# Gates and values of a hybrid attention layer: token-major seven-product blocks in place of weight pairs

## The chip, the cores and the metric

The kernel runs on one core of a Trainium2 chip. The metric is the device time of one launch in microseconds (us). Engines are called by the profile's names: PE is TensorE (matmuls), DVE is VectorE, ACT is ScalarE, POOL is GpSimd and SP is the engine that issues most DMAs.

## The reference, cut to what matters

One layer on 512 tokens of width 2048, float32. One projection of the normalised input makes nine things; two token mixers, latent attention (A) and a spatial gating unit (B), are gated, added and projected.

```python
h = rmsnorm(x, attn_norm_g) * (1 + scale) + shift        # shift, scale, gate = silu(c) @ w_ada + b_ada
q_lat, kv_lat, k_rope, z_mla, u, v, z_sgu, g_mla, g_sgu = split_cols(h @ w_in)   # 768 512 64 and six of 2048
y_mla = causal_mla_attention(...) * silu(z_mla)          # 16 heads of 128, softmax over 512 keys
y_sgu = u * (tril(w_s) @ rmsnorm(v) + b_s) * silu(z_sgu) # 16 groups of 128 columns, chunks of 128 tokens
merged = sigmoid(g_mla) * y_mla + sigmoid(g_sgu) * y_sgu
x = x + gate * (merged @ w_out); return rmsnorm(x)
```

In the kernel the column groups are called by letters: z and g are `z_mla` and `g_mla` (16 heads of 128 columns each), u, s and t are `u`, `z_sgu` and `g_sgu`, v is `v`.

## The kernel before, in words

**Arithmetic.** Every float32 operand is split into a high part (a cast, on ACT) and a low part (a subtraction, on DVE), both in the type `fp32r`; a product is three matmuls, high by high, high by low and low by high (`mm3`, lines 143 to 146). A weight granule of 1024 columns therefore costs one ACT cast and one DVE subtraction before PE can use it. `Stream` (`ws`) loads, splits and hands out granules in a fixed order, one granule split ahead and three loaded ahead.

**Stages on PE, in order.** (1) `g1`: 16 granules for the first 1024 columns of `w_in` (the latents). (2) `g2`: 16 granules for 640 columns. Beside these two, DVE computes the dot products of silu(c) with `w_ada` (`ada_dot`, one 128x2048 tile each) and `fix_to` turns the inputs into the final h, split into `hh[j]`, `hl[j]`. (3) The plain stage (`gb`): two granules of 1024 columns for g of head 14, and v's upper 1024 columns with `k_rope`'s 64 in three column groups of 384, 384 and 320 columns, tokens on the partitions. Four more dots (`NG = 4`) run here. (4) The blocks: seven `BLOCKS`, each a 2x2 block product done with seven products in place of eight. A block takes two groups of 512 columns, for instance v's first two. Its list `V7` has 28 slots; in a slot a weight granule meets 12 matmuls of 512 columns, with tokens stationary (token-major: tokens on the partitions of the result). The sums of h's quarters that the seven products need are made once (`make_sums`, `sums`). (5) The pairs: 14 pairs of weight granules (`PAIRS`), z or g of two neighbouring heads, by the same seven products, but with the weights stationary and 256 tokens moving, 98 slots of 24 or 16 matmuls; the result has features on the partitions, as attention wants it. (6) Attention, head by head. (7) The output projection in four column groups of 512 with the residual, gate and final norm; twelve more dots of the gate run here.

**Who orders the rest.** The order is written out by hand and nothing reorders it. In stages 4 and 5 small jobs (mixing of B, rotary tables, norms of the latents, biases from `shift`) are put into slots by `on(slot, phase, f)`; `place` looks for a slot in which the DVE time noted so far leaves room. Slots of the blocks count up to -1, those of the pairs from 0. In a slot the phases run in the order FIRST, HIGH (cast of the granule of two slots later), EVAC, GATE, SPLIT (its low part), BACK, then the matmuls, then MISC and LOAD. `lat_split` makes the high and low parts of the ten latent tiles that attention reads.

**Attention for one head.** `scores`, `softmax` (mask, maximum and exponentials; `normalise` multiplies the probabilities by 1/sum on DVE), the next head's query projection (`qproj`, and for even heads the rotary part of the next pair, `rproj`), ten `transposes` of the probabilities and their splits, `kproj` of the next head, `turn` (four transposes of B's part), `pv`, `merge_a` (times the gate `gt[h]`, plus B's part), and for odd heads `vproj`. The banks of PSUM go round in a ring of seven.

Of the kernel before, what the change touches and what calls it, by code (L numbers as in the profile page):

```python
# [37 lines left out]
GATED = "ust"  # L38
VW = (384, 384, 320)
VC = (1024, 1408, 1792)  # L40
# [7 lines left out]
DOTS = (3, 3, 4, 5, 5, 6, 7, 8, 9, 9, 10, 11, 11, 12, 12, 13, 13, 14, 14, 15, 16, 16, 16, 16, 16)  # L48
FIXED = (0, 0, 0, 0, 2, 2, 2, 2, 2, 4, 4, 4, 6, 6, 8, 8, 10, 10, 12, 12, 14, 14, 16, 16, 16)

SHIFT_AT = (17, 18, 19, 20, 21, 22, 23, 24, 25, 27, 28, 30, 31, 33, 34, 36)

# [13 lines left out]
class Stream:  # L66
# [17 lines left out]
    def dma_to(self, i):  # L84
        i = min(i, len(self.src) - 1 if self.limit is None else self.limit)
        while self.n_dma <= i:
            k = self.n_dma
            for f in self.before.pop(k, ()):
                f()
            ap, n, _ = self.src[k]  # L90
            pool, tag = self.raws[self.next_raw]
            self.next_raw = (self.next_raw + 1) % len(self.raws)
            t = pool.tile([P, GW], F32, tag=tag, name=f"{tag}_{k}")
            for o, m, ap_ in ap if isinstance(ap, list) else [(0, n, ap)]:
                (self.first if k == 0 else self.nc.sync).dma_start(t[:, o:o + m], ap_)
            self.raw[k] = t
            self.n_dma += 1
# [27 lines left out]
def trunk_layer(ctx, tc, xT, xn, c, vecs, pos, wada, w1, w2, wv, wv3, wv4, wh, wh15, wq, wqr, wk, wvv, wo, wsT, bsp, gfin, out,  # L125
# [82 lines left out]
    ssv = nt(cst, [P, NB, 5], F32, "ssv")  # L208
    rv = nt(cst, [P, NB], F32, "rv")
    cosT = nt(latp.p, [P, S], F32, "cosT")  # L210
# [9 lines left out]
    z_d = scratch("z_d", [P, S])  # L220
    v_d = scratch("v_d", [NB, P, D])
    kr_d = scratch("kr_d", [NB, P, 64])
# [4 lines left out]
    g_d = [scratch(f"g_d{i}", [8, P, S]) for i in range(2)]  # L227
# [34 lines left out]
    def third_place():  # L262
        return [nt(c1[0].p, [P, GW], F32R, tag) for tag in ("w2h", "w2l")]


    steps = [("z", 0)] + [(0, i) for i in range(8)] + [("z", 1)] + [(cg, i) for cg in (1, 2) for i in range(8)]
    gb = []
    for cg, i in steps:
        if cg == "z":
            gb.append(ws.add(wh[H - 2, 1, i], GW))  # L270
        else:
            last = (cg, i) == (2, 7)
            gb.append(ws.add((wv3[0], wv3[1], wv4)[cg][i], 2 * VW[cg], to=third_place if last else None))
# [41 lines left out]
    ada = Scope("ada", side=RIGHT)  # L315
    xp = Scope("xT")
# [25 lines left out]
    xt = [nt(xp.p, [P, S], F32, f"x{j}") for j in range(KC)]  # L342
# [29 lines left out]
    for j in range(NG):  # L372
        load_before(gb[8 + j], ada_load, 2 * KC + j)
# [5 lines left out]
    def square_of(j):  # L379
# [3 lines left out]
        sq = nt(xp.p, [P, S], F32, "sq", bufs=2)  # L383
# [58 lines left out]
    n_fix = 0  # L442

    def fix_to(n, between=None):

        nonlocal n_fix
        if n_fix >= min(n, KC):
            if between:
                between()
            return  # L450
        js = range(n_fix, min(n, KC))
        assert n_dot >= js[-1] + 1
        n_fix = js[-1] + 1
        cols = slice(js[0], n_fix)
        tt(shift[:, cols], dots[:, cols], vec[:, C_BADA + js[0]:C_BADA + n_fix], ALU.add)
        ts_ = []
        for j in js:
            t = nt(xp.p, [P, S], F32, "t", bufs=2)
            stt(t, xt[j], gxA[:, j:j + 1], rx, ALU.mult, ALU.mult)
            ts_.append(t)  # L460
        for j, t in zip(js, ts_):
            hh[j] = nt(hp.p, [P, S], F32R, f"hh{j}")
            ACT.activation(hh[j], t, AF.Identity, bias=shift[:, j:j + 1])
        if between:
            between()
        for j, t in zip(js, ts_):
            hl[j] = nt(hp.p, [P, S], F32R, f"hl{j}")
            stt(hl[j], t, shift[:, j:j + 1], hh[j].bitcast(F32), ALU.add, ALU.subtract)

    ws.split_to(g2[0])  # L470
    for m in range(8):
        ACT.copy(lat[m], ps1[m])
# [7 lines left out]
    for j in range(KC):  # L480
        wH, wL = get(g2[j])
# [3 lines left out]
        if j < NB:  # L485
            DVE.reciprocal(out=rx[:, j * P:(j + 1) * P], in_=rx[:, j * P:(j + 1) * P])
        dot_to(DOTS[j])
        fix_to(FIXED[j])
    for m in range(5):
        pend.append(lambda m=m: ACT.copy(lat[8 + m], ps2[m]))  # L490
# [7 lines left out]
    def parts_of(name, c):  # L498

        if name in sums:  # L500
            return sums[name][:, c, 0], sums[name][:, c, 1]
        return sums[name + "h"][:, c], sums[name + "l"][:, c]

    def split_sum(name, j, src):
        hilo(*parts_of(name, j), src)

    def half_of(tags, j):

        if j % 2 == 0:
            halves_[tags, j // 2] = slot(tags[j // 2])  # L510
        return halves_[tags, j // 2][:, (left, right)[j % 2]]

    halves_, s3f, s4f = {}, {}, {}
    S3_AT, S4_AT = ("lat8", "lat9", "lat12", "lat7"), ("lat0", "lat1", "lat2", "lat3")

    def make_sums(j):
        a, b = (nt(tb.p, [P, S], F32, f"t{i}") for i in range(2))
        tt(a, hh[j].bitcast(F32), hl[j].bitcast(F32), ALU.add)
        tt(b, hh[j + 8].bitcast(F32), hl[j + 8].bitcast(F32), ALU.add)
        s3f[j], s4f[j] = half_of(S3_AT, j), half_of(S4_AT, j)  # L520
        tt(s3f[j], a[:, left], a[:, right], ALU.subtract)
        tt(b[:, right], a[:, right], b[:, right], ALU.subtract)
        tt(a[:, left], b[:, right], a[:, left], ALU.subtract)
        tt(s4f[j], a[:, left], b[:, left], ALU.add)
        return lambda: (split_sum("s1", j, b[:, right]), split_sum("s2", j, a[:, left]))


    made, leaving = [], []

    def store(dst, src):  # L530
        made.append((dst, src))

    def stores():
        for dst, src in leaving:
            DMA.dma_start(dst, src)
        leaving[:], made[:] = made[:], []

    def lat_scale(i):
        tt(lat[i], lat[i], rx, ALU.mult)
        store(lat_d[i], lat[i])  # L540

    for n, i in enumerate((8, 0, 9, 12, 1, 10, 11, 2, 7, 3, 4, 5, 6)):
        early.setdefault(9 + n // 2 if n < 4 else 7 + n, []).append(lambda i=i: lat_scale(i))

    def sums_begin(j, at_):
        early.setdefault(at_ + 1, []).insert(0, make_sums(j))

    for j in range(8):
        at_ = 11 + 2 * j
        early.setdefault(at_, []).append(lambda j=j, at_=at_: sums_begin(j, at_))  # L550

    def evac_v(n, cg, ps):
        m = VW[cg] // P
        w, c0 = m * P, VC[cg]
        if n < 2:
            t = nt(tb.p, [P, S], F32, "sig", bufs=2)
        elif cg == 0:
            t = nt(c1[0].p, [P, GW], F32, f"raw{2 + n}")
        else:
            t = slot("lat10" if n == 2 else "lat11" if cg == 1 else "lat6")  # L560
        ACT.activation(t[:, :w], ps[:, :w], AF.Square, accum_out=ssv[:, n, cg:cg + 1])
        ACT.copy(t[:, :VW[cg]], ps[:, :VW[cg]])
        store(v_d[n][:, c0:c0 + w], t[:, :w])
# [1445 lines left out]
```

## Time and profile before

| what | value |
|---|---|
| median of 3 runs | 1580.8 us (1579.93 to 1580.96) |
| the profiled execution's own time | 1578.76 us |
| its span in the profile | 1577.0 us |
| granted PE clock, mean | 0.998 |
| PE busy | 1562.0 us, 8461 matmuls |
| DVE, ACT busy | 1234.6 us, 766.4 us |
| DMA | 318.37 MB, mean 202 GB/s |

The span runs from the first to the last instruction; the execution's own time is 1.8 us longer, and the median of the runs 2.0 us longer again. A matmul's duration in the trace is modelled and overlaps its neighbours, so matmuls are counted here over a stretch of time and not by their durations. The stages of before, by the trace: `g2` ends at about 155.8 us, the plain stage at 261.5, the blocks at 812.1, the pairs at 1096.3, the last head at about 1400, the last matmul at 1568.9.

### The profile page before, as it was taken

How to read it: one execution, taken by the hardware profiler on the slowest of the kernel's cores; microseconds unless marked ns; L12 is line 12 of the kernel's file. 1: busy time of each engine (PE TensorE's matmuls, PEld its weight loads, DVE VectorE, ACT ScalarE, POOL GpSimd, SP SyncE). 2: the span in 40 equal slices, each digit the busy share in tenths (PEclk: the TensorE clock that was granted, in tenths of full speed). 3: DMA queues.
4: the chain of work that ended last, by engine and by line, in shares of the span. 5: the costliest groups of instructions: out<-in, count | busy, mean ns of one | idle time of the engine just before them, and what ended most of it. 6: DMA issues, size and time to landing. Idle time of an engine off the chain costs nothing.

```text
span 1577.0 us, 22523 instructions
## 1 busy us (share of the span) xinstructions
PE 1562.0 (99%) x8461; PEld 1360.4 (86%) x8461; DVE 1234.6 (78%) x1747; ACT 766.4 (49%) x1220; POOL 79.0 (5%) x86
## 2 busy tenths in 40 slices
PE   8999999999999999999999999999999999999997
PEld 7888999888888888888889999999888888888886
DVE  8989888777978797878788777777777777757763
ACT  4343335555555464555464456646544545532232
POOL 0000000010101000201001111110000000000000
PEclk9999999999999999999999999999999999999999
DMA  9979557585868777868759898886322223249722
GB/s 380 365 257 326 224 179 242 154 237 150 227 194 231 204 213 217 223 180 226 211 175 253 214 246 228 246 213 191 126 91 84 84 92 99 78 176 364 277 91 107
DMA packets 182975, 318.37 MB, mean 202 GB/s; under 512 B 14361, under 2 KB 118353, under 8 KB 176081
## 3 DMA queue, kind: packets, MB, share of 16 engines
q1 hardware_dynamic: 162706, 281.28, 52.1%
q0 software_dynamic: 20016, 35.13, 13.4%
q8 instruction: 66, 1.08, 0.3%
q10 hardware_dynamic: 144, 0.52, 0.1%
q14 instruction: 43, 0.35, 0.1%
HBM read 293.47 MB, written 23.42 MB: 201 GB/s over the span
## 4 chain that ended last, share of the span: by engine, by line
PE 94%; DVE 2%; ACT 2%; DMA 1%; issue 1%; DVEq 0%; ACTq 0%
PE ps L145 14%; PE ps L146 14%; PE ps L144 14%; PE ps L1533 10%; PE ps L1531 10%; PE ps L1532 10%; PE ps L1557 6%; PE ps L1555 4%; PE ps L1556 4%; PE ps L1553 3%; PE ps L1722 1%; DVE raw L132 1%; PE ps L1685 1%; PE ps L1686 1%; DMA wada<-in_wada 1%
## 5 line engine op out<-in xcount | busy, mean ns | idle before, releaser
L135 DVE SCALAR_TENSOR_TENSOR wada<-wada,cact 128x2048 f32<-128x2048 f32 x47 | 107.2, 2282 | 2.3 <-DMA wada<-in_wada 2.3
L114 ACT CAST w1h<-wraw 128x1024 fp32r<-128x1024 f32 (+3 forms) x65 | 54.9, 844 | 102.2 <-PE ps L146 46.8
L132 DVE TENSOR_TENSOR w2l<-raw,w2h 128x1024 fp32r<-128x1024 f32 x65 | 79.5, 1223 | 29.2 <-ACT w2h L621 15.2
L114 ACT CAST w0h<-wraw 128x1024 fp32r<-128x1024 f32 (+3 forms) x66 | 60.4, 915 | 77.9 <-PE ps L146 33.7
L132 DVE TENSOR_TENSOR w1l<-raw,w1h 128x1024 fp32r<-128x1024 f32 x61 | 74.6, 1223 | 25.4 <-ACT w1h L621 17.3
L115 DVE TENSOR_TENSOR w0l<-wraw,w0h 128x1024 fp32r<-128x1024 f32 (+3 forms) x66 | 69.2, 1048 | 30.4 <-ACT w0h L114 30.1
L132 DVE TENSOR_TENSOR w0l<-raw,w0h 128x1024 fp32r<-128x1024 f32 x62 | 75.8, 1223 | 21.7 <-ACT w0h L621 15.7
L144 PE MATMUL ps<-hh,w1h 128*128 128x512 f32 x226 | 90.1, 399 | 1.1 <-ACT hh L419 1.0
L145 PE MATMUL ps<-hl,w1h 128*128 128x512 f32 x226 | 88.2, 390 | 0.5 <-DVE hl L135 0.5
L146 PE MATMUL ps<-hh,w1l 128*128 128x512 f32 x226 | 88.4, 391 | 0.0
L132 DVE TENSOR_TENSOR d<-ps,d 128x256 f32<-128x256 f32 (+2 forms) x130 | 72.5, 571 | 17.6 <-ACT d L149 13.0
L115 DVE TENSOR_TENSOR w1l<-wraw,w1h 128x1024 fp32r<-128x1024 f32 (+3 forms) x65 | 62.5, 962 | 29.3 <-ACT w1h L114 28.2
L144 PE MATMUL ps<-hh,w0h 128*128 128x512 f32 x198 | 77.9, 394 | 0.0
L146 PE MATMUL ps<-hh,w0l 128*128 128x512 f32 x198 | 77.3, 390 | 0.0
L145 PE MATMUL ps<-hl,w0h 128*128 128x512 f32 x198 | 77.2, 390 | 0.0
L621 ACT CAST w0h<-raw 128x1024 fp32r<-128x1024 f32 x44 | 46.3, 1051 | 62.7 <-PE ps L1532 37.6
L621 ACT CAST w1h<-raw 128x1024 fp32r<-128x1024 f32 x45 | 47.3, 1052 | 56.3 <-PE ps L1532 38.3
L621 ACT CAST w2h<-raw 128x1024 fp32r<-128x1024 f32 x44 | 46.3, 1052 | 49.3 <-PE ps L1532 27.7
L144 PE MATMUL ps<-w0h,hh 128*128 128x256 f32 (+2 forms) x224 | 67.8, 303 | 0.0
L132 DVE TENSOR_TENSOR w1l<-wraw,w1h 128x1024 fp32r<-128x1024 f32 x37 | 45.3, 1224 | 28.3 <-ACT w1h L783 13.2
L146 PE MATMUL ps<-w0h,hl 128*128 128x256 f32 (+2 forms) x224 | 67.5, 301 | 0.0
L145 PE MATMUL ps<-w0l,hh 128*128 128x256 f32 (+2 forms) x224 | 67.4, 301 | 0.0
(428 smaller groups left out, 5127.9 us busy)
## 6 DMA issues: line engine op xcount, KB each, us to landing
raw<-in_wh SPq DMA_DIRECT2D x120, 512.0 KB, 5.2
wada<-in_wada SPq DMA_DIRECT2D x47, 1024.0 KB, 7.4
wraw<-in_wh POOLq DMA_DIRECT2D x35, 512.0 KB, 8.0
wraw<-in_wo SPq DMA_DIRECT2D x32, 512.0 KB, 4.6
wraw<-in_wh SPq DMA_DIRECT2D x30, 512.0 KB, 5.7
raw<-in_wh POOLq DMA_DIRECT2D x20, 512.0 KB, 6.9
raw<-in_wv SPq DMA_DIRECT2D x17, 512.0 KB, 3.2
raw<-in_wh SPq DMA_DIRECT2D x22, 384.0 KB, 5.1
```

Source lines behind the costliest of these rows:

```text
L114: self.nc.scalar.copy(hi[:, :n], raw[:, :n])
L115: self.nc.vector.tensor_tensor(out=lo[:, :n], in0=raw[:, :n], in1=hi[:, :n].bitcast(F32), op=ALU.subtract)
L132: DVE.tensor_tensor(out=out, in0=in0, in1=in1, op=op)
L135: DVE.scalar_tensor_tensor(out=out, in0=in0, scalar=scalar, in1=in1, op0=op0, op1=op1, **kw)
L144: PE.matmul(ps, ah, bh, start=start, stop=False)
L145: PE.matmul(ps, ah, bl, start=False, stop=False)
L146: PE.matmul(ps, al, bh, start=False, stop=stop)
L621: ACT.copy(hi, t)
L1531: PE.matmul(ps[t].rearrange("p (h w) -> p h w", h=4), xh[:, tk], wH[:, k], start=st, stop=False, skip_group_check=True)
L1532: PE.matmul(ps[t].rearrange("p (h w) -> p h w", h=4), xl[:, tk], wH[:, k], start=False, stop=False, skip_group_check=True)
L1533: PE.matmul(ps[t].rearrange("p (h w) -> p h w", h=4), xh[:, tk], wL[:, k], start=False, stop=sp, skip_group_check=True)
L1557: PE.matmul(ps, wL[:, sl], xh, start=False, stop=sp, skip_group_check=True)
```

## The change

z and g of heads 0 to 11 leave the pairs and become three more blocks of four heads each, token-major; v's upper half becomes a block too. So there are eleven blocks (308 slots) and no pairs. z and g of heads 12 and 13 and `k_rope` join g of head 14 in the plain stage, which becomes 16 granules of 704 columns with the weights stationary. The gates of heads 0 to 11 now lie with tokens on the partitions: ACT multiplies them by 1/sum there (four instructions of 128 columns), PE transposes them, ACT copies them out of PSUM, and the probabilities of these heads are not normalised any more. Eight of the gate's dots (`NG = 8`) are cut into 32 pieces of 512 columns and run in attention, two a head, the other eight in the output projection; none runs in the plain stage. The latents are stored unscaled and scaled when they are read back; h is fixed in pairs of tiles; the sums are made from pairs of tiles.

```diff
-PAIRS = [((t, h), (t, h + 1)) for h in range(0, 14, 2) for t in "zg"]
-BLOCKS = [("v", 0, "v", 1)]
+BLOCKS = [("v", 0, "v", 1), ("v", 2, "v", 3)]
 for c_ in (0, 2):
     BLOCKS += [("u", c_, "s", c_), ("t", c_, "u", c_ + 1), ("s", c_ + 1, "t", c_ + 1)]
-VW = (384, 384, 320)
+BLOCKS += [("z", c_, "g", c_) for c_ in range(3)]
+GATED = 12
-NG = 4
+NG = 8
+FIX_AT = (6, 9, 12, 16, 18, 20, 22, 24)
...
+    def plain_at(j):
+        cols = slice(j % 8 * P, (j % 8 + 1) * P)
+        pairs = [(n * 2 * P, 2 * P, wh[H - 4:H - 2, n, j // 8][:, :, cols].rearrange("h p x -> p h x")) for n in range(2)]
+        kr_ = wv4[j // 2][:, j % 2 * 320 + 256:(j % 2 + 1) * 320]
+        return pairs + [(4 * P, P, wh[H - 2, 1, j // 8][:, cols])] + [(5 * P, 64, kr_)]
+    gb = [ws.add(plain_at(j), 5 * P + 64, to=third_place if j == KC - 1 else None) for j in range(KC)]
...
+    def lat_out(m, ps):
+        ACT.copy(lat[m], ps)
+        store(lat_d[m], lat[m])
...
-    for st, (cg, i) in enumerate(steps):
+    for st in range(KC):
...
+        for m in range(6):
+            sl = slice(m * P, min((m + 1) * P, 5 * P + 64))
+            mm3(plain[m], wH[:, sl], wL[:, sl], hh[st], hl[st], st == 0, st == KC - 1)
...
     def squash(key):
-        ACT.activation(held[key], held[key], AF.Silu if key[0] == "s" else AF.Sigmoid)
+        ACT.activation(held[key], held[key], AF.Silu if key[0] in "sz" else AF.Sigmoid)
+    def g_gate(c, half):
+        z = held["z", c, half]
+        tt(z, z, held["g", c, half], ALU.mult)
+    def g_out(c, half):
+        DMA.dma_start(gt_d[c][2 * half:2 * half + 2].rearrange("n p w -> p n w"), held["z", c, half])
...
+    s_att = max(V7.index((2, 3)) + 1 - n_v, s_lat + 1)
+    on(s_att, LOAD, to_attention)
+    for i in range(10):
+        on(s_att + i // 2, LOAD, lat_fetch, i)
+        on(V7.index((3, 3)) + 1 - n_v + i // 2 if i < 8 else -4, BACK, lat_split, i)
...
-    for s, (p, k) in enumerate(order):
...
-            PE.matmul(ps, wL[:, sl], xh, start=False, stop=sp, skip_group_check=True)
...
+    def piece_load(i):
+        q, j = pieces[i]
+        pieces_of[i] = nt(gd.p, [P, S], F32, "piece", bufs=4)
+        DMA.dma_start(pieces_of[i], wada[2 * KC + j][:, q * S:(q + 1) * S])
+    def piece_sum(i):
+        q, j = pieces[i]
+        t = pieces_of.pop(i)
+        stt(t, t, 1.0, cq[q], ALU.mult, ALU.mult, accum_out=partial[:, j, q:q + 1])
...
         def normalise(i):
             DVE.reciprocal(out=mx[:, 4 + i:6 + i], in_=mx[:, 8 + i:10 + i])
-            for q in (i + 1, i):
-                ts(pr_[q], pr_[q], mx[:, 4 + q:5 + q], None, ALU.mult)
+            if h >= GATED:
+                for q in (i + 1, i):
+                    ts(pr_[q], pr_[q], mx[:, 4 + q:5 + q], None, ALU.mult)
...
+        if h % 2 and h < H - 1:
+            pieces_at(h)
         normalise(0)
...
         pa, fa = transposes(pr_, (0,))
         fa()
+        if h < GATED:
+            for n in range(NB):
+                g_ = gt[h][:, n * P:(n + 1) * P]
+                ACT.activation(g_, g_, AF.Copy, scale=shares_[:, n:n + 1])
         pb, fb = transposes(pr_, (1,))
...
-        tps = turn(h)
+        gate_ = gt[h]
+        if h < GATED:
+            gate_ = nt(tp, [P, S], F32, "sig", bufs=3)
+            ACT.copy(gate_, turn(gt[h]))
+        tps = turn(vt[h])
         ops = pv(h, {**pa, **pb, **pc})
-        merge_a(h, ops, tps)
+        merge_a(h, ops, tps, gate_)
+        if not odd:
+            pieces_at(h)
...
-    chunk_at = dict(zip(range(NG, KC), (2, 3, 4, 5, 6, 8, 9, 10, 11, 12, 13, 14)))
+    chunk_at = dict(zip(range(NG, KC), (5, 7, 9, 10, 11, 12, 13, 14)))
```

More of the change, by code (lines that the diff above doesn't have):

```diff
@@ L528, in trunk_layer @@
[L528 to L558, printed above, removed]
-        else:
[L560 to L563, printed above, removed]
-        if cg == 2:
-            store(kr_d[n], t[:, w:VW[cg]])
@@ L567, in evac_z, with split_sums @@
-    def evac_z():
-        t = nt(tb.p, [P, S], F32, "sig", bufs=2)
-        ACT.copy(t, plain)
-        store(z_d, t)
-    kept_at = [(lambda: c1[0].p, "raw7")] + [(lambda: wp, f"wraw{i}") for i in (1, 2, 0)]
+        if name == "s4":
+            return sums[name][c // 2][:, c % 2, 0], sums[name][c // 2][:, c % 2, 1]
+        return sums[name][:, c, 0], sums[name][:, c, 1]
+    def split_sums(name, k, src):
+        hi, lo = (sums[name][k][:, :, e] if name == "s4" else sums[name][:, 2 * k:2 * k + 2, e] for e in range(2))
+        hilo(hi, lo, src)
@@ L1827, in trunk_layer @@
     merge()
+    DVE.tensor_reduce(out=dots[:, 2 * KC:2 * KC + NG], in_=partial, axis=AX.X, op=ALU.add)
+    gate_sum(0, NG)
+    gate_store(0, NG)
+    gd.close()
     hp.close()
```

701 lines of the change are left out of this document (289 added, 412 removed).

## The prediction

> **What bounds the kernel.** I read the page first, then the busy time by stretches, cut at the borders of the stages, then the groups by line and the timeline of one pair of heads and of the passage into attention. From the page:
>
> ```profile
> span 1577.0 us, 22523 instructions
> PE 1562.0 (99%) x8461; PEld 1360.4 (86%) x8461; DVE 1234.6 (78%) x1747; ACT 766.4 (49%) x1220; POOL 79.0 (5%) x86
> PE 94%; DVE 2%; ACT 2%; DMA 1%; issue 1%; DVEq 0%; ACTq 0%
> ```
>
> PE works for 99% of the span, and 94% of the chain that ended last is PE. Nothing but fewer or cheaper matmuls can shorten this kernel by much, and whatever makes PE wait adds its whole length. The busy time by stretches (time, then busy time and count of each engine, clock, DMA share, GB/s) gives the stages and, in its last two rows, two stretches of matmuls of one width:
>
> ```profile
> core 0: us, PE busy (x) PEld busy (x) DVE busy (x) ACT busy (x) POOL busy (x), PEclk, DMA share, GB/s
> 100.96:155.80 54.84, 54.84 (x242) 45.23 (x241) 50.59 (x63) 19.32 (x27) 0.00 (x0) 1.00 0.88 315
> 155.80:161.25 5.45, 5.45 (x26) 4.50 (x24) 5.06 (x8) 3.69 (x6) 0.00 (x0) 1.00 0.92 335
> 161.25:194.55 33.30, 33.30 (x193) 33.30 (x192) 26.64 (x32) 12.05 (x16) 0.00 (x0) 1.00 0.59 218
> 194.55:200.03 5.48, 5.48 (x25) 4.51 (x25) 4.98 (x7) 1.82 (x5) 0.00 (x0) 1.00 0.35 128
> 200.03:233.34 33.31, 33.31 (x194) 33.30 (x192) 26.92 (x47) 11.75 (x24) 0.00 (x0) 1.00 0.61 189
> 233.34:261.49 28.15, 28.15 (x193) 28.15 (x193) 23.08 (x46) 12.44 (x28) 0.00 (x0) 1.00 0.70 244
> 261.49:812.06 550.57, 548.16 (x2409) 449.56 (x2408) 452.31 (x530) 294.58 (x416) 44.11 (x37) 1.00 0.73 204
> 812.06:1096.30 284.24, 284.24 (x2147) 272.69 (x2147) 217.10 (x277) 157.37 (x216) 32.68 (x39) 1.00 0.84 225
> 1096.30:1383.00 286.70, 286.36 (x1682) 253.22 (x1681) 226.47 (x472) 153.74 (x331) 0.00 (x0) 1.00 0.30 96
> 582.00:649.50 67.50, 67.32 (x297) 55.44 (x296) 57.46 (x61) 32.22 (x39) 3.85 (x3) 1.00 0.80 233
> 879.04:890.68 11.64, 11.64 (x99) 11.63 (x97) 7.86 (x10) 5.80 (x8) 2.56 (x3) 1.00 0.62 164
> ```
>
> A 512-column matmul comes every 67.50/297 = 0.227 us. In the last row, 97 matmuls of 256 columns and two cut at the edges: 11.64/97 = 0.120. So two of 256 cost 0.240 where one of 512 costs 0.227: 13 ns for every matmul beside its columns. Only in the blocks is PE idle at all (550.57 against 548.16).
>
> **The change part by part.** Counted from the code, the changed products stream 811,008 columns before and after: v's upper half gains the eighth that z and g of heads 12 and 13 lose. What falls is their number, from 2,704 to 1,584, and 1,120 times 13 ns is 14.6 us. By stages:
>
> Plain stage: 5.45 + 33.30 + 5.48 + 33.31 + 28.15 = 105.7 us goes. In its place come 16 steps of 18 matmuls of 512 columns: 288 x 0.227 = 65.4. Gain 40.3.
>
> Pairs: 1,904 matmuls of 256 columns (228.5) and 224 of 512 (50.8) are 279.3 of the stage's 284.24; the rest is 19 other matmuls, which nearly all stay, and small waits. I take a gain of 281.4, between the two.
>
> Blocks: the 550.57 us hold 196 slots, 45 matmuls of B's mixing (10.2) and some dozen transposes (1.2): 539.2/196 = 2.751 us a slot, where 12 matmuls alone are 2.724. The 112 new slots cost 308.1 at the measured rate, 305.1 without any wait. I take the first: the planner fills the new slots with DVE work no thinner than it did the old ones.
>
> Gates turned on PE: twelve heads, four transposes each. The timeline has B's:
>
> ```profile
> 1165.74 0.60 PE L1748 MATMUL ps<-ident,b 128*128 128x128 f32 x4
> 1166.10 0.47 PE L144 MATMUL ps<-hh,d 128*128 128x512 f32 x1
> ```
>
> 1166.10 - 1165.74 = 0.36 us, twelve times 4.3. Sum so far: -40.3 - 281.4 + 308.1 + 4.3 = -9.3 us (-12.3 with no wait in the new slots).
>
> By the Trainium skill (TensorE: Matmul & The Clock Gate, "Back-to-back issue gap") a warm matmul costs its columns at 2.4 GHz and a fixed 2.5 ns. By that rule the 1,120 matmuls are worth 2.8 us and not 14.6. This trace disagrees: 13 ns.
>
> What goes beside PE, at nothing: DVE and ACT drop the pairs' splits and sums (217.1 and 157.4 us of busy time in a stage of 284.2) and take up as much a slot in the new blocks. In `g2` nine stores of 256 KB are added to SP's queue, ahead of weights; the stage ran at 315 GB/s and a DMA share of 0.88, and 2.4 MB more in 54.84 us are 43 GB/s: it fits narrowly while DVE loses a fix there. If the cover is gone the dots come late and a few us are lost; I keep 0 to 3. The four dots taken out of the plain stage, and four of twelve out of the projection, stand off the path. On SP each piece's reload waits for an earlier piece on DVE, and the next weights stand behind it; weights come three granules ahead, 42 matmuls or more (9.5 us), so DVE would have to be that late.
>
> New waits, first: the odd heads of attention. After `merge_a` of an even head DVE now does two pieces before it can mask the next, odd head's scores. The rows of one odd head, with the price of a piece from the groups by line (a 128x512 instruction of the same kind) and of its read-out:
>
> ```profile
> 1132.70 0.29 DVE L132 TENSOR_TENSOR ps<-ps,mask 128x128 f32<-128x128 f32 x1
> 1136.99 0.20 ACT L1706 ACTIVATION_READ_ACCUMULATOR hl<-ps,mx 128x1 f32 x1
> 1137.43 0.55 DVE L139 TENSOR_SCALAR hl<-hl,mx 128x256 f32<-128x256 f32 x2
> 1138.53 0.38 PE L1722 MATMUL ps<-ident,hl 128*128 128x128 f32 x2
> ...
> L135 DVE SCALAR_TENSOR_TENSOR rx<-half,shift,rx 128x512 f32<-128x512 f32 x30 | 22.4, 746 | 0.0
> 16.76 0.08 DVE L135 DVE_READ_ACCUMULATOR wada<-wada,cact 128x1 f32 x1
> ```
>
> Today the probabilities are ready at 1137.98 and PE turns them at 1138.53: 0.55 us to spare, with no gap before the mask at 1132.70. Two pieces are 1.65, some 1.5 as DVE's instructions overlap by a tenth. Without `normalise` the exponentials alone count: 1137.19 + 1.5, + 0.36 as `pv` comes after one more turn, is 1139.05; PE arrives at 1138.53 + 0.36 = 1138.89. Wait 0.16, six times 1.0. Head 13 keeps `normalise` and follows two pieces: 1137.98 + 1.5 - 1138.53 = 0.95. Together 1.9 (0 to 5, the end at which each odd head waits 0.7). Queued behind are DVE's low parts for `pv`, which PE reads five us later.
>
> Second: the passage into attention. The last five slots of the blocks that hold `lat_split` (-8 to -4) have it unplanned. Prices:
>
> ```profile
> L1459 ACT ACTIVATE hh<-b,vec 128x512 fp32r<-128x512 f32 x10 | 6.5, 709 | 0.0
> L135 DVE SCALAR_TENSOR_TENSOR hl<-b,vec,hh 128x512 fp32r<-128x512 f32 x10 | 7.0, 749 | 0.0
> L132 DVE TENSOR_TENSOR w0l<-raw,w0h 128x1024 fp32r<-128x1024 f32 x45 | 55.0, 1223 | 17.2 <-ACT w0h L621 15.7 <-PE ps L1532 1.2
> 1132.10 0.69 DVE L132 TENSOR_TENSOR sig<-sig,ps 128x512 f32<-128x512 f32 x1
> L1039 ACT ACTIVATE d<-d 128x1024 f32<-128x1024 f32 x16 | 16.9, 1057 | 0.1
> L1039 ACT ACT_TABLE_LOAD x5 | 6.4, 1283 | 0.1
> 1101.70 2.35 ACT L1429 COPY hl<-ps 32x512 f32<-32x512 f32 x4
> 1104.08 0.62 ACT L114 CAST w1h<-wraw 128x512 fp32r<-128x512 f32 x1
> ```
>
> DVE has there ten `lat_split` lows (7.5), five granules' lows and three sums (eight at 1.22: 9.8) and four of 0.69 (2.8): 20.1 us in five slots of 2.75, 13.8. The low part of a granule has two slots of lead, and PE needs it only for the third matmul, 0.45 in; slots -3 and -2 are light. Following the lows one by one PE waits some 0.15 in slot -2 and 0.5 in -1. Then ACT: after the last slot it casts `gq[0]` (0.84 for 768 columns, between the 0.62 and the 1.05 of its neighbours), empties two banks (1.2), loads a table (1.28), squashes twice (2.1) and casts the key (0.6), 6.0, before the rotary copies of 2.35 and the cast of `gk[0]`, all in its queue: 9.0, its low at 9.7. PE is there after 36 matmuls, 8.2, plus 0.45: a wait of 1.05, where the same copies cost some 0.45 before. Together 1.3 (0 to 4).
>
> Sum: -9.3 + 1.9 + 1.3 = -6.1. The profiled execution took 1578.76 us (span 1577.0 and 1.8 around it), 2.0 under the median of the runs; I apply the difference to the median: 1574.7 us.
>
> **The rivals.** (a) No new wait: margins of tenths turn out the other way and the new slots run at 2.724. -12.3, 1568.5 us. For it: the waits above are each under one us. Against: the old blocks do wait, 6 us in 550. Chance 0.12.
>
> (b) Slower: ACT falls behind in the twelve gated heads. The four scalings stand in its queue between the first cast of the transposes and all that `pv` and the next head's scores read:
>
> ```profile
> L1087 ACT ACTIVATE lat<-lat,rv 128x128 f32<-128x128 f32 x64 | 20.5, 393 | 0.0
> 1129.07 0.59 ACT L149 CAST d<-ps 128x512 fp32r<-128x512 f32 x1 [1.31 <-PE ps L146]
> ```
>
> 4 x 0.393 = 1.57 us, then 0.6 for the copy of the turned gate. The key's cast, next in the queue, waited 1.31 for PE at 1129.07, so 0.26 is late, against 0.36 that PE itself comes later, and ACT is busy for only 153.74 of 286.70. It decides when more than 6.1/12 = 0.5 us a head reaches PE; at 1 us a head it is +12: 1586.7. Chance 0.14.
>
> (c) One price a column: the new matmuls of 512 gain nothing by being fewer, since the 13 ns belong to the stages that go and not to each matmul. Then 14.6 us are missing: 1589.3. Against it stand the two rows above, each from another stage, and the 192 matmuls of 384 columns at 33.30/192 = 0.173, on the same line between them. Chance 0.04. By the fixed 2.5 ns of the Trainium skill (same page and section) 11.8 of the 14.6 us would be missing, 1586.5; the trace's rows speak against it.
>
> **How the numbers follow.** My forecast, 0.70, spans 1568 to 1580 with the bounds above. 0.2% (3.2 us, about what a measurement of this kernel can tell from no change) puts "faster" under 1577.6: 0.60 of my 0.70 lie there, 0.08 within 0.2%, 0.02 above. With (a) faster has 0.72; with a small case of (b) same has 0.10; (b) and (c) make slower 0.18. The range 1568 to 1584 leaves out a few hundredths below and the full cases of (b) and (c).
>
> **What would show it.** Right: about 7,390 matmuls, none of 256 or 384 columns outside attention; a plain stage of 65 to 67 us; eleven blocks in 852 to 862; a pair of heads some 0.7 to 1.1 us longer than 36.9. Wrong: PE idle at `pv` or scores in each gated head (b); a slot of the new blocks over 2.85 us; a plain stage over 70, where dots or stores come late; several us between the last slot and the first scores.

## The result, and the profile after

The changed kernel takes **1594.34 us** (median of 4 runs, 1592.18 to 1595.34) where the kernel before takes 1580.37 (median of 4 runs, 1579.02 to 1580.96): a ratio of 1.0088, with a 95% interval of 1.007 to 1.0105. It is slower by 14 us. The forecast was 1574.7 us, 6 us less than before; its range ended at 1584.

The profiled execution took 1595.34 us, with a span of 1593.6. From its page, the busy time, and the shares by engine and by line of the chain of work that ended last:

```profile
span 1593.6 us, 20601 instructions
PE 1563.6 (98%) x7397; PEld 1299.8 (82%) x7397; DVE 1220.5 (77%) x1662; ACT 801.4 (50%) x1238; POOL 69.5 (4%) x67
PE 38%; DMA 4%; DVE 3%; ACT 2%; issue 1%; SPq 0%; DVEq 0%; ACTq 0%
PE ps L148 7%; PE ps L149 7%; PE ps L147 7%; PE ps L1367 5%; PE ps L1365 5%; PE ps L1366 5%; DMA wraw<-in_wo 2%; DMA gate_row<-gate 1%; PE ps L1574 1%; PE ps L1600 1%; PE ps L1534 1%; PE ps L1535 1%; DVE X L135 1%; DMA b<-latn_d 0%; DVE wada L138 0%
```

The matmuls fell from 8,461 to 7,397, close to the 7,390 forecast. But the chain now holds 4% of DMA, and two transfers have a share of 1% or more: the output projection's weights (`in_wo`) and `gate_row`, the DRAM scratch through which the final gate is turned from columns into a row. The prediction has no word on `gate_row`. The stages (time, busy time and count of each engine, clock, DMA share, GB/s) are `g2`, the plain stage, the blocks, attention up to head 15's first transposes, and from there to the last matmul:

```profile
101.20:156.00 54.80, 54.80 (x242) 45.20 (x241) 47.39 (x55) 24.17 (x35) 0.00 (x0) 1.00 0.94 337
156.00:221.85 65.85, 65.85 (x290) 51.52 (x289) 50.39 (x70) 32.68 (x48) 0.00 (x0) 1.00 0.59 182
221.85:1087.01 865.16, 859.78 (x3781) 705.20 (x3780) 702.88 (x797) 472.64 (x617) 67.36 (x56) 1.00 0.74 206
1087.01:1377.13 290.12, 289.21 (x1713) 255.61 (x1711) 220.53 (x463) 169.58 (x384) 0.00 (x0) 1.00 0.40 126
1377.13:1585.89 208.76, 197.23 (x899) 161.70 (x897) 110.38 (x162) 55.68 (x90) 0.00 (x0) 0.97 0.51 169
```

The last stage of the kernel before, by the same view of its trace:

```profile
1379.47:1568.90 189.43, 189.21 (x902) 158.01 (x900) 115.89 (x160) 55.79 (x90) 0.00 (x0) 1.00 0.55 206
```

At head 15's transposes the changed kernel is 2.3 us ahead (1377.13 against 1379.47). Then it needs 208.76 us for the work that took 189.43: PE idles for 11.5 us, and is busy for 8.0 us more with the same products, at a granted clock of 0.97. The loss of 19.3 us is all made there. What PE waited for in that stage (line waited for, us in total, times, longest), one of ACT's waits there, and of SP's queue the waits behind `gate_row`:

```profile
PE ps L147 <- ACT w0h L117: 5.6, 2, 3.2
PE ps L147 <- ACT w1h L117: 2.5, 1, 2.5
PE ps L148 <- DVE w0l L118: 2.0, 3, 0.8
PE ps L148 <- DVE w1l L118: 1.2, 2, 0.8
...
ACT w0h L117 <- DMA wraw<-in_wo: 21.6, 4, 11.9
...
SPq L1710 <- DMA gate_row<-gate: 21.6, 3, 10.1
```

PE waits for the high part of a weight granule, hence for ACT; ACT in turn for weights still on their way. The queue of SP shows what held them (start, duration, line, transfer):

```profile
1411.28 0.38 SPq L670 DMA_DIRECT2D gate_row<-gate  x1
1421.85 0.80 SPq L1710 DMA_DIRECT2D gbc<-gate_row  x2
1422.74 0.38 SPq L1742 DMA_DIRECT2D gfb<-in_gfin  x1
1423.17 0.42 SPq L1705 DMA_DIRECT2D cact<-cact_d  x1
1423.69 0.38 SPq L98 DMA_DIRECT2D wraw<-in_wo  x1
```

SP issues a store at 1411.28 and nothing for 10 us, until it has landed and may be read back (`gbc`). Then the loads queued behind go out together. The lines responsible are a part of the change that the diff above leaves out and the prediction passes over:

```diff
-    def gate_turn(a, b, pg, row):
-        PE.transpose(pg[:b - a, :P], gate[:, a:b], ident)
-        DVE.tensor_copy(row[:b - a, :P], pg[:b - a, :P])
-        return lambda: DMA.dma_start(gate_row[a:b], row[:b - a, :P])
+    def gate_store(a, b):
+        DMA.dma_start(gate_row[a:b].rearrange("k p -> p k"), gate[:, a:b])
```

Before, four gate columns were turned on PE and stored as rows of 512 bytes. Now the columns go to DRAM as they lie, one element of 4 bytes at a time: three stores of 1,024, 512 and 512 elements, all in the output projection.

### The profile page after: what moved, and what is told of

It reads as the page before. It is cut to its first block, busy times and chain, and to the rows that moved or that the text cites. A ratio compares the mean times of both kernels' runs of the same rounds, so it can differ in the third digit from the quotient of the medians.

```text
span 1593.6 us, 20601 instructions
## 1 busy us (share of the span) xinstructions
PE 1563.6 (98%) x7397; PEld 1299.8 (82%) x7397; DVE 1220.5 (77%) x1662; ACT 801.4 (50%) x1238; POOL 69.5 (4%) x67
## 2 busy tenths in 40 slices
DMA packets 239288, 316.16 MB, mean 198 GB/s; under 512 B 18281, under 2 KB 186257, under 8 KB 233553
## 5 line engine op out<-in xcount | busy, mean ns | idle before, releaser
L135 DVE TENSOR_TENSOR X<-X,X 128x1024 fp32r<-128x1024 f32 (+2 forms) x110 | 129.4, 1181 | 29.5 <-ACT X L620 26.6
L147 PE MATMUL ps<-hh,w1h 128*128 128x512 f32 (+1 forms) x260 | 103.4, 398 | 1.7 <-ACT hh L425 1.4
L148 PE MATMUL ps<-hl,w1h 128*128 128x512 f32 (+1 forms) x260 | 101.6, 391 | 0.5 <-DVE hl L138 0.5
L149 PE MATMUL ps<-hh,w1l 128*128 128x512 f32 (+1 forms) x260 | 101.5, 391 | 0.0
L1367 PE MATMUL ps<-w1l,hh 128*128 128x512 f32 x236 | 92.3, 391 | 2.5 <-DVE w1l L135 2.5
L1367 PE MATMUL ps<-w0l,hh 128*128 128x512 f32 x236 | 92.3, 391 | 1.8 <-DVE w0l L135 1.7
L1365 PE MATMUL ps<-w0h,hh 128*128 128x512 f32 x236 | 92.1, 390 | 0.1
L1365 PE MATMUL ps<-w1h,hh 128*128 128x512 f32 x236 | 91.9, 390 | 0.2 <-ACT w0h L620 0.2
L1366 PE MATMUL ps<-w0h,hl 128*128 128x512 f32 x236 | 91.9, 389 | 0.0
L1366 PE MATMUL ps<-w1h,hl 128*128 128x512 f32 x236 | 91.9, 389 | 0.0
```

The lines of the kernel that those rows point to most:

```text
L135: DVE.tensor_tensor(out=out, in0=in0, in1=in1, op=op)
L147: PE.matmul(ps, ah, bh, start=start, stop=False)
L148: PE.matmul(ps, ah, bl, start=False, stop=False)
L149: PE.matmul(ps, al, bh, start=False, stop=stop)
L1365: PE.matmul(ps[t].rearrange("p (h w) -> p h w", h=4), xh[:, tk], wH[:, k], start=st, stop=False, skip_group_check=True)
L1366: PE.matmul(ps[t].rearrange("p (h w) -> p h w", h=4), xl[:, tk], wH[:, k], start=False, stop=False, skip_group_check=True)
```

## The experiments

Each ratio is to the kernel before, run on the same chip; the brackets hold its 95% interval. Where a diff or a fence leaves lines out, `...` marks it; of a diff, only the lines that matter for the reading are shown.

**e1: the rows stored as before.** Theory A is SP's blocked queue, theory B the changed bunching of loads, theory C a loss made earlier. (Theory D, that the small pieces hold up the other transfers, comes with e2.)

```diff
-    gate_store(0, NG)
...
+    for a, b, st, k in ((0, NG, 1, 4), (NG, NG + 4, 11, 0), (NG + 4, KC, 17, 4)):
+        later.setdefault(st, []).append(lambda a=a, b=b, k=k: rows.append(
+            gate_turn(a, b, bank_at(k), nt(tp, [P, S], F32, "sig", bufs=3))))
+        later.setdefault(st + 1, []).append(lambda: rows.pop()())
+        for cg in range(a // 4, b // 4):
+            later.setdefault(st + 2, []).append(lambda cg=cg: grow_load(cg))
```

> The changed kernel, with its gate rows turned on TensorE and stored row by row as in the kernel before (eight rows in step 1 of the output projection, four in steps 11 and 17), and each read back a step after its store is issued. Theory A (SP's one queue waits 21.6 us in three waits for stores of 4-byte elements to land, the loads behind them come late and in a burst, and TensorE waits for weights): the waits of SP for gate_row fall under 2 us each, the excess over the matmuls' own spacing in the output stage falls from 19.6 us to about 1.5, and the time is 1575 to 1578 us. Theory B (the loads bunch because the gain, the eight gate rows and y now ask for the queues together, however the rows are stored): 1588 to 1594. Theory C (the loss is made in the blocks and in attention, and only shows at the end): 1593 to 1595.

Measured: 1578.75 us, 0.9997 [0.9988, 1.0007]. The loss is gone. In the windows of its trace the last stage takes 190.82 us, PE busy for 189.85 of them:

```profile
1378.75:1569.57 190.82, 189.85 (x902) 157.92 (x900) 111.10 (x165) 56.30 (x90) 0.00 (x0) 1.00 0.53 185
```

That puts the loss on the store, with everything tied to it, and rules out C; B too, as far as it holds however the rows are stored. It doesn't separate SP's waiting from what the store does to its neighbours. SP's waits fell to 8.0 us in three, not under 2 each as A had it. That was the first hint.

**e2: the stores on another queue.**

```diff
-        DMA.dma_start(gate_row[a:b].rearrange("k p -> p k"), gate[:, a:b])
+        nc.gpsimd.dma_start(gate_row[a:b].rearrange("k p -> p k"), gate[:, a:b])
...
-        DMA.dma_start(grow[:, cols], ...
+        nc.gpsimd.dma_start(grow[:, cols], ...
```

> The changed kernel, its stores of 4-byte elements kept as they are, but these three stores and the four loads that read the rows back are issued on GpSimd's queue, so that SP has nothing to wait for. Theory A (SP's waiting): the store still takes some 10 us to land, SP waits for none of it, and the time is 1575 to 1579 us. Theory D (the 4-byte stores themselves hold up the transfers beside them): the late weights stay, and the time stays at 1588 to 1595. Theory B (bunched loads): 1588 to 1594 too, but with no wait of SP before the bunch.

Measured: 1589.65 us, 1.0073 [1.0057, 1.009]. **e3: the reading back put later.**

```diff
+    for cg, st in ((0, 3), (1, 4)):
+        later.setdefault(st, []).append(lambda cg=cg: grow_load(cg))
...
-        later.setdefault(st + 2, []).append(lambda cg=cg: grow_load(cg))
+        later.setdefault(st + 4, []).append(lambda cg=cg: grow_load(cg))
...
-    for cg in range(NG // 4):
-        grow_load(cg)
```

> The changed kernel, its stores of 4-byte elements kept on SP; only the loads that read the rows back are put later in program order (steps 3 and 4 of the output projection in place of its start, and two steps more behind the two later stores). Theory A: the store has landed when SP comes to the loads, SP's waits for gate_row fall from 21.6 us to under 4, and the time is 1575 to 1580 us. Theory D (the stores' own traffic): 1588 to 1595. Theory B (bunched loads): 1585 to 1594.

Measured: 1591.86 us, 1.0082 [1.0067, 1.0097]. Theory A, my first, falls: with SP's wait gone (e2) or down to 3.5 us (e3) most of the loss stays. The traces say why. First, of e2, SP's waits for weights in this stage (it has none for `gate_row` left), and the window of the third store on GpSimd's queue; then e3's windows, the 11 us behind the 1,024-element store and the 9.7 behind the third; then two stretches of e1 at the same places, with the same kinds of loads under way:

```profile
SPq L98 <- DMA wraw<-in_wo: 15.2, 6, 6.5
...
1494.60:1503.80 9.20, 8.30 (x37) 6.55 (x35) 5.20 (x6) 1.66 (x3) 0.76 (x1) 1.00 1.02 31
```

```profile
1411.20:1422.20 11.00, 11.00 (x51) 9.09 (x50) 3.60 (x3) 2.11 (x2) 0.00 (x0) 1.00 0.89 54
1504.30:1514.00 9.70, 9.70 (x45) 8.02 (x44) 5.96 (x8) 4.13 (x7) 0.00 (x0) 1.00 0.57 111
```

```profile
1409.00:1422.00 13.00, 13.00 (x62) 10.79 (x61) 5.17 (x9) 3.67 (x4) 0.00 (x0) 1.00 0.90 311
1504.30:1514.00 9.70, 9.70 (x45) 7.92 (x44) 7.25 (x10) 3.73 (x7) 0.00 (x0) 1.00 0.59 203
```

At a DMA share of 0.89 the engines move 54 GB/s beside the store of 4-byte elements, where they move 311 without it; at the third store it is 111 against 203, and 31 in e2. What is in flight then is held: a granule of `in_wo` issued at 1503.95, just ahead of e3's third store, lands after 9.2 us; in e1 such a granule, issued at 1503.90, takes 3.6. So theory D: the store holds its neighbours for as long as it lasts, on SP's queue as on GpSimd's. By the Trainium skill (DMA: Bandwidth & Descriptors, "Issuing engines are not separate DMA queues") transfers issued on SP and on GpSimd end on the same 16 engines and interleave; e2, at 1589.65 us, agrees.

The busy share of these windows is the neighbours' and not the store's own. In the changed kernel SP issues nothing beside the first store, and the window shows it alone:

```profile
1411.30:1421.80 10.50, 10.50 (x48) 8.69 (x47) 3.58 (x3) 2.11 (x2) 0.00 (x0) 1.00 0.07 2
```

A share of 0.07, and 10.5 us to land all the same. The trace has 1,040 packets under 512 bytes in that time, and none of them starts after 1413, 1.7 us behind the issue. So it is not its packets' time on the engines that makes the store last; what it waits for in the other nine us no run here shows.

**e8: the same stores in larger pieces.** This is the disputed cost by itself: queue, place and number of stores as in the change, and only the layout in DRAM differs (so the gate's values come back in another order).

```diff
-        DMA.dma_start(gate_row[a:b].rearrange("k p -> p k"), gate[:, a:b])
+        DMA.dma_start(gate_row[a:b].rearrange("k p -> (k p)").rearrange("(p k) -> p k", k=b - a), gate[:, a:b])
```

> The changed kernel, its three stores on the same queue at the same places, but each partition's gate values lie together in DRAM: 128 pieces of 32 or 16 bytes in place of 1,024 or 512 of 4 (the gate's rows so come out in another order, and the output with them). Theory D (many small pieces hold up the transfers): the stores land in 3 to 5 us, the transfers beside them are not held, and the time is 1575 to 1580. Theory A (SP waits behind any store that it must see landed): some 3 us of wait are left each time, 1579 to 1584. Theory B (bunched loads): 1588 to 1594.

Measured: 1578.54 us, 0.9992 [0.9982, 1.0001]. The time of landing, min/median/max, over the `gate_row` transfers of e8 (three stores and four loads), and the same line of the changed kernel:

```profile
DMA to landing us min/median/max: 1.4/3.8/5.0
```

```profile
DMA to landing us min/median/max: 3.4/10.6/11.5
```

The 1,024-element store that took 10.5 us lands in 1.4 as 128 pieces of 32 bytes, and the whole loss goes. So the cause, shown, is the layout of 4-byte pieces. By the Trainium skill (DMA: Bandwidth & Descriptors, "Rules for kernel authors") a transfer whose last dimension isn't contiguous becomes one descriptor per element, to be avoided by a rearrangement. On SP's queue the traces agree: the page of the changed kernel has 18,281 packets under 512 bytes and that of e1 16,201, and the three stores have 2,048 elements. On GpSimd's queue (e2) the page has only 16,281, and the loss is there all the same; so the cost does not go by the packets that the page counts.

**e4: the same store in the kernel before**, whose order of loads is another.

```diff
-    on(10, MISC, lambda: gate_turn(0, NG, bank(), sig())())
+    on(10, MISC, lambda: gate_store(0, NG))
...
+    for n, st in enumerate((9, 11, 17)):
+        a = NG + 4 * n
+        later.setdefault(st + 1, []).append(lambda a=a: gate_store(a, a + 4))
```

> The kernel before, with its four row stores of the gate (turned on TensorE) made as stores of 4-byte elements instead, four gate columns of 128 each; nothing else of the change. Theory D (a store of 4-byte elements holds up every transfer in flight for some 10 us): each of the four takes 9 to 12 us to land, the transfers beside it land 5 to 10 us later than before, and the three in the output projection cost 6 to 14 us: 1585 to 1593 us. Theory B (the changed order of the loads is what hurts): within 1 us of the kernel before, 1578 to 1580.

Measured: 1589.63 us, 1.0064 [1.0051, 1.0078]: ten us from these lines alone. Its first store in the output projection lands after 12.8 us, SP waits behind two of them,

```profile
SPq L1841 <- DMA gate_row<-gate: 18.6, 2, 11.1
```

and PE stands still once, from 1490.6 on, for 7.2 us. The change's order isn't needed for the loss; theory B is out. Its first element store, in the blocks, took 15.8 us, longer than the 9 to 12 expected, and cost nothing that shows: the last stage takes 199.30 us against 189.43, which is all of the ten.

**e7: two stores joined.** The two later stores of 512 elements become one of 1,024, behind the last dot.

```diff
+    st = chunk_at[KC - 1]
+    later.setdefault(st + 1, []).append(lambda: gate_store(NG, KC))
     for cg in range(NG // 4, 4):
-        st = chunk_at[4 * cg + 3]
-        later.setdefault(st + 1, []).append(lambda cg=cg: gate_store(4 * cg, 4 * cg + 4))
```

> The changed kernel, its two later stores of 512 elements of 4 bytes made as one of 1,024 after the last dot. If the hold is paid for each store (10.5, 11.5 and 10.6 us for 1,024, 512 and 512 elements in the changed kernel say so), one hold of some 10 us falls away and the time falls by 3 to 6 us, to 1588 to 1591. If it is paid for each element, the joined store takes about 20 us and the time stays at 1592 to 1596.

Measured: 1592.28 us, 1.0081 [1.0067, 1.0095], against 1.0088 for the change: the intervals lie over each other. The joined store takes 11.9 us to land, where one of 512 took 11.5, so the hold goes by the store rather than by the element at these sizes. Yet hardly any time came back: this one falls among other loads and costs PE 3.1 us at one place. How long a store holds and what that costs are two things.

**The smaller stalls.** e1 is where the prediction, put right on the store, should have come out at 1574.7, and it took 1578.75. Its trace has five other stalls, known already from the changed kernel's waits of PE from the end of the blocks to head 15:

```profile
PE ps L1367 <- DVE w0l L135: 1.4, 1, 1.4
PE ps L1367 <- DVE w1l L135: 1.3, 1, 1.3
PE ps L148 <- DVE w0l L118: 0.8, 1, 0.8
PE ps L1574 <- DVE hl L142: 0.6, 1, 0.6
PE ps L147 <- ACT w1h L117: 0.3, 1, 0.3
```

**e5** moves only the splits of the latents:

```diff
-        on(V7.index((3, 3)) + 1 - n_v + i // 2 if i < 8 else -4, BACK, lat_split, i)
+        on((-8, -7, -6, -5, -4, -3, -2, -2, -2, -1)[i], BACK, lat_split, i)
```

> The changed kernel, with the ten splits of the normalised latents in the last block spread over slots -8 to -1, one a slot but two in slot -2, in place of two a slot in -8 to -4. Theory E (VectorE, with two splits a slot beside the low parts, falls behind and the lag of 3.2 us at the block's end is its lateness): the stalls at slots -5 and -3 go, and the time falls by 2 to 3 us, to 1591.5 to 1592.5. Theory F (the late loads of the latents hold the chain up, the order does not matter): the lag stays within 0.5 us and the time at 1594. If the last splits come late for the first projection of attention instead, up to 1 us of it comes back there.

Measured: 1593.75 us, 1.0096 [1.008, 1.0111]: no gain by the time. The edit puts three splits into slot -2, where the expectation has two. In the trace both waits in the blocks are gone, and one of 2.0 us is there at the passage:

```profile
PE ps L149 <- DVE w1l L118: 2.0, 1, 2.0
```

With one split a slot no wait is left in the blocks; the four splits in the last two slots come ahead of the low part of the first attention weights and, by my reading, delay it. **e6** moves on from e1, with a denser spread and three pieces of the dots later:

```diff
+        on((-8, -8, -7, -7, -6, -5, -4, -3, -3, -2)[i], BACK, lat_split, i)
...
             merge()
-            pieces_at(h)
             out_granule(0, 2, pso)
+            pieces_at(h)
```

> The row stores of e1_row_store, and two edits for the stalls that are left there: the ten splits of the normalised latents lie at slots -8, -8, -7, -7, -6, -5, -4, -3, -3 and -2 of the last block (two a slot only where VectorE had idle time), and the last three pieces of the gate's dots come behind the third granule of the output projection instead of ahead of it. Theory E: the stalls of 1.55 and 1.48 us in the block go without coming back at the passage, and so does that of 1.03 us in head 15: 3 to 4 us off, 1574.5 to 1576. Rival: VectorE has no time left there, the 2.1 us that came back at the passage in e5_lat_spread stay, and only the 1.0 us of the pieces goes: 1577.5 to 1578.

Measured: 1577.43 us, 0.9984 [0.9976, 0.9993]. By its trace neither edit did what I expected: the waits are 1.0 and 1.1 us in the blocks and 1.3 at the passage, and the 0.8 us in head 15 are still there. I had moved the wrong pieces. DVE's timeline of the changed kernel shows it:

```profile
1385.09 0.69 DVE L138 SCALAR_TENSOR_TENSOR piece<-piece,cq 128x512 f32<-128x512 f32 x1
...
1385.70 0.69 DVE L138 SCALAR_TENSOR_TENSOR piece<-piece,cq 128x512 f32<-128x512 f32 x1
...
1386.31 0.68 DVE L138 SCALAR_TENSOR_TENSOR piece<-piece,cq 128x512 f32<-128x512 f32 x1
1386.93 0.08 DVE L138 DVE_READ_ACCUMULATOR piece<-piece,cq 128x1 f32 x1
1386.93 0.29 DVE L135 TENSOR_TENSOR ps<-ps,mask 128x128 f32<-128x128 f32 x1
```

The three pieces ahead of head 15's mask at 1386.93 are those of head 14, issued behind its merge. (In the code heads 14 and 15 have three pieces each and head 13 none, not two a head throughout.) **e9** moves these, and those of head 12:

```diff
+        if i < 7:
+            on(i - 8, BACK, lat_split, i)
...
     rps = rproj(0)
+    for i in range(7, 10):
+        lat_split(i)
...
+        if h == H - 3:
+            pieces_at(12)
...
-            pieces_at(h)
+            pieces_at(14)
             out_granule(0, 2, pso)
...
     merge()
+    pieces_at(15)
```

> The row stores of e1_row_store (the first a step later), and: seven splits of the latents at slots -8 to -2, one a slot, the last three behind the first projection of attention, which does not read them; and the six pieces of the gate's dots that lay ahead of the masks of heads 13 and 15 put behind head 13's softmax, ahead of the third output granule, and behind the last merge. If VectorE's queue at these places is the cause of the stalls left in e1_row_store (1.55 + 1.48 in the block, 0.50 at the passage, 0.74 at head 13, 1.03 at head 15), 4 to 5 us go: 1574 to 1575.5 us. If late loads of the latents cause those in the block, only the 1.8 us of heads 13 and 15 go: 1576.5 to 1577.5.

Measured: 1576.88 us, 0.9985 [0.9976, 0.9994]. The waits at heads 13 and 15 are gone, so they were the pieces. But at the passage PE now waits 1.3 us for the cast of the key weights, where it was 0.3, which I put down to the three splits behind the first projection, and 0.6 for a granule's low part. A further wait, of 1.3 us at 1445.9, stands behind a whole dot (2.28 us on DVE); why only this run has it I have not followed. **e11** takes what held from each:

```diff
+        if i < 9:
+            on((-8, -7, -6, -5, -4, -3, -2, -2, -1)[i], BACK, lat_split, i)
...
     rps = rproj(0)
+    lat_split(9)
...
+        if h in (13, 14):
+            pieces_at({13: 12, 14: 14}[h])
...
-        if not odd:
+        if h < 12 and not odd:
             pieces_at(h)
```

> The row stores of e1_row_store, the latents' splits at slots -8 to -1 (one a slot, two in slot -2) with the last behind the first projection of attention, and the five pieces of the gate's dots that lay ahead of the masks of heads 13 and 15 put behind the transposes of heads 13 and 14; the last three stay where the change has them. If these two stalls (0.74 and 1.03 us) are VectorE's queue of pieces, they go. If half of the block's end lag of 3 us and the passage's 0.5 go too, the time is 1575.5 to 1577 us; if the lag only moves on, as in e6_row_lat_pieces, 1577 to 1577.5.

Measured: **1573.58 us**, 0.996 [0.9946, 0.9973], 5.8 us under the kernel before on its chip and better than expected. PE's waits, from the blocks' end to the last matmul, are two:

```profile
PE ps L149 <- DVE w1l L118: 1.3, 1, 1.3
PE ps L1371 <- DVE w1l L135: 0.6, 1, 0.6
```

```profile
223.34:1085.67 862.33, 859.17 (x3781) 705.24 (x3780) 700.04 (x793) 472.12 (x616) 67.36 (x56) 1.00 0.75 207
1085.67:1375.98 290.31, 288.99 (x1713) 255.75 (x1711) 223.57 (x467) 170.21 (x385) 0.00 (x0) 1.00 0.42 126
1375.98:1565.45 189.47, 189.25 (x902) 158.01 (x900) 110.75 (x165) 55.88 (x90) 0.00 (x0) 1.00 0.54 186
```

Its blocks are 2.8 us shorter than the changed kernel's (862.33 against 865.16), and its last stage is that of the kernel before (189.47 against 189.43). In attention 290.31 against 290.12 are no gain: the passage costs more, head 13 less. ACT's longest wait for a latent's load is 2.3 us here and 2.0 in the changed kernel: most of the lag in the blocks went (0.6 us of waits is left of 2.7) though ACT still waits as long for these loads, so it was DVE's order and not the loads.

**e10: the price of a matmul.** From e1, with each 512-column matmul of the z and g blocks cut in two. The sums of z and g differ from the reference's in this kernel; instructions and data moved are as told.

```diff
+                    for e in (slice(0, 4),) if b < G0 else (slice(0, 2), slice(2, 4)):
+                        o = ps[t].rearrange("p (h w) -> p h w", h=4)[:, e]
+                        PE.matmul(o, xh[:, tk], wH[:, k, e], start=st, stop=False, skip_group_check=True)
...
```

> The disputed cost by itself: e1_row_store with each of the 1,008 matmuls of 512 columns in the three z and g blocks made as two of 256, so 1,008 more matmuls and the same columns. By this case's rows (227 ns for 512 columns, 120 for 256) each pair takes 13 ns more: 13.1 us more than e1_row_store, 1591 to 1593 us. By the fixed 2.5 ns a matmul of the Trainium skill (TensorE: Matmul & The Clock Gate, section on the back-to-back issue gap): 2.5 us more, about 1581. By one price a column (the rival that put the change at 1589): nothing more, 1578.5 to 1579.5.

Measured: 1587.41 us, 1.0051 [1.0037, 1.0065], so 8.5 us over e1 by the ratios, under the 13.1 expected but far from 2.5 or nothing. The same 70 us of the z blocks, first in e10, then in e1 (here PE alone is listed):

```profile
880.00:950.00 70.00, 70.00 (x586) 1.00 0.71 201
```

```profile
880.00:950.00 70.00, 69.95 (x309) 1.00 0.74 212
```

70/586 is 0.1195 us, 70/309 is 0.2265: two halves cost 12 ns more than a whole. The 1,008 of them, 12 to 13 us, show up as 10.2 us in the block stage (875.3 against 865.1) and as 8.5 in all. In that stage PE waits some 1.3 us less than in e1, and is busy for 11.7 us more (871.5 against 859.8). The step from 10.2 to 8.5 lies ahead of the blocks: e1's profiled execution has a granted clock of 0.50 from 19.5 to 22.9 us, e10's has not, and they reach the blocks at 223.5 and 221.7. The price belongs to the matmul and not to the stage, and one price a column is refuted. The fixed 2.5 ns of the Trainium skill (TensorE: Matmul & The Clock Gate, "Back-to-back issue gap"), which the page gives for the isolated gap of a single matmul, is not the price in this kernel.

## Why the prediction was wrong

**The step that failed** is the list of what the change adds. Under "what goes beside PE, at nothing", the prediction takes the dots in the output projection as "off the path". It never looks at the stores and loads that carry these dots to the residual, nor at the row store that had become an element store. The term is missing from the sum. It measured 19.3 us between the profiled executions (189.43 to 208.76), which lie 16.6 us apart where the medians lie 14.0; taken out again, it is 14 to 15 us by e1's and e8's ratios against the change's. Two parts, as far as e2 separates them: SP's own wait, 2 to 7 us (e2 against the change, by the ratios and by the last stage's 201.62 us against 208.76), and the hold of other transfers, 11 to 13 (201.62 against e8's 190.30, and by the ratios). The trace of before has row stores alone, so no row of it gave this store's price; the diff showed that it was coming.

**Mis-sized: the end of the blocks.** The lag was put at 0.65 us. The trace has waits of 1.4 and 1.3, and 2.8 us came back in e11. The load was right, 20 us of DVE work in slots for 14, but I followed only the lows of the last slots and let the slots at which the splits themselves lie pass as covered by two slots of lead. For the eleven blocks I had written 852 to 862 us: 865.16. The passage's term was too large: 0.3 us of waiting instead of 1.05. For head 15 there was no term: its mask stands behind three pieces, and PE waits 0.8 us there.

**Right:** g2 54.80 us (0 to 3 us more were allowed). The plain stage 65.85, forecast 65.4. The price of 13 ns a matmul, on which the gain rests. Attention grew by 6.95 us from the blocks' end to head 15 (283.17 to 290.12); forecast 6.85, but by parts that differ. A pair of heads takes 37.87 us against 36.89. A turned gate costs some 0.5 us a head (half of the 0.98 by which a pair grew) instead of 0.36, the wait forecast for six odd heads isn't there, and head 13's is 0.6 instead of 0.95. So the sum agreed partly by luck.

At head 15 the forecast lead was 6.1 us and the real one 2.3. Of the 3.8 missing, some 2.6 are the end lag; the others are tenths (0.7 in g2 and the plain stage, 0.4 in the blocks' slots).

**The rivals.** (a) fell with the lag. (b), ACT behind in the gated heads: from 1087 to 1345 us PE's only wait is the passage's 0.3. (c) fell with e10. None of them named a transfer: all three looked at PE, DVE and ACT, and "slower" had 0.18 for mechanisms that did not come. With the store set right and DVE's jobs spread, the kernel takes 1573.58 us on its chip, close to the forecast of 1574.7: the gain argued from matmuls is there, and the store and the order of DVE's jobs hid it. That the figures come so close is partly luck, since the waits in the forecast (1.9 us in attention, 1.3 at the end of the blocks and the passage) are not those that e11 has left (0.6 in the blocks, 1.3 at the passage).

## What to carry to other kernels

List every transfer that the change touches, with the size of its smallest contiguous piece at both ends: a store whose pieces became 4 bytes cost 14 to 15 us here, about what 1,120 matmuls fewer brought (14.6 at 13 ns). Look at the GB/s and the DMA share together: a share of 0.89 at 54 GB/s was transfers that were held, beside a store that had a share of 0.07 when alone. And when jobs are moved into a queue that executes in order, find out ahead of which instruction they land: the pieces sat two statements away from where I looked for them.

## What the runs showed of the hardware

A store of 512 or 1,024 elements of 4 bytes took 9 to 13 us to land in the output projection of six kernels (the changed one, e2, e3, e4, e5 and e7), little depending on the count, alone (10.5 us with nothing else issued) or beside others. The same bytes in 128 pieces took 1.4 to 5 us.

A long wait of PE cost more than its length. The changed kernel's three longest waits (3.2, 2.5 and 2.4 us) are each followed by a granted clock of 0.50 for 3.4 or 6.8 us. First two windows of it, behind the first and the third, then one of e5, behind its wait of 2.0 us at the passage (the clock stands ahead of the DMA share):

```profile
1435.30:1438.60 3.30, 3.30 (x10) 2.52 (x9) 0.00 (x0) 0.33 (x1) 0.00 (x0) 0.50 1.03 431
1523.40:1527.40 4.00, 4.00 (x11) 3.13 (x10) 3.16 (x4) 2.45 (x4) 0.00 (x0) 0.50 0.42 129
```

```profile
1088.30:1091.50 3.20, 3.20 (x9) 2.51 (x8) 3.08 (x4) 2.42 (x3) 0.00 (x0) 0.50 0.58 173
```

11 matmuls in 4.00 us, where 4.00/0.227 would be 17 or 18: 1.5 us lost in this window, and 1.0 and 1.2 in the others, on top of the waits. Behind the waits of 1.3 us in e9 and e11 the clock stayed at 1.00. But the length of one wait doesn't decide it: in e5 a wait of 1.1 us and, 0.5 us later, one of 0.8 (ending at 1522.7 and 1523.9) were followed by a clock of 0.50 from 1525.1 to 1528.5. By the Trainium skill (TensorE: Matmul & The Clock Gate, "Part 1: The HAM clock gate") the clock falls to half after an idle window of some 3.4 us. Half and 3.4 us agree with the record here (0.50, for 3.4 us or twice that), but a wait of 2.0 us was already enough.
